# Feed forward 0 of a two-layer trunk: squares of half 2 first, table constants later, each piece's phases behind its C table, and three smaller edits

## The chip, the cores and the metric

The kernel runs on one core of a Trainium2 chip. TensorE multiplies matrices, VectorE, ScalarE and GpSimd work element by element, SyncE issues most DMAs. The profile calls them PE (PEld for its weight loads), DVE, ACT, POOL and SP. The metric is the device time of one execution in microseconds (us), the median of several runs; lower is better.

## The reference

A causal decoder trunk of two layers on x of 1024 tokens by 1024 channels, all in float32. What matters here is the feed forward and the S5 mixer:

```python
for i in range(DEPTH):
    h = h + mix_fns[i % 2](rms_norm(h, norm_mix[i]), *mix_params[i])
    h = h + sqrelu_mlp(rms_norm(h, norm_ffn[i]), *ffn[i])     # square(relu(hn @ up)) @ down, 4096 wide
    gate = jax.nn.sigmoid(rms_norm(h, norm_ple[i]) @ ple[i][0])
    h = h + (p[i] @ ple[i][1]) * gate
return rms_norm(h, norm_final)
```

Mixer 0 is RWKV-7 beside a short convolution. Mixer 1 is S5: 64 groups of 16 channels with 64 complex states each, a diagonal recurrence over time, then a GLU.

## The kernel before, in words

The residual h lies in SBUF as 8 x 2 tiles `h[j][hf]` of 128 channels by 512 tokens; hf 0 ("half 1" of the tokens, named `ha` in the profile) and hf 1 ("half 2", named `h`). Every matrix product is made of three matmuls of float32r parts: high by high, high by low, low by high (`mm3`, L161). The high part is a cast on ACT, the low part a subtraction on DVE or POOL.

The stages run one after the other: mixer 0, feed forward 0, layer 0's gate product (`ple`), S5 with its GLU, feed forward 1, `ple` of layer 1 with the final norm (`finish`).

**Feed forward** (`ffn`, L253) is a list of units k = -6, -5, ... Each unit has 8 slots. In a unit the up product of weight block k+5 takes 24 matmuls, and from k = 0 the down product of block k takes another 21, in a Strassen-like form with sums of the weight's quarters. Work on the other engines is queued with `at(k, slot, f)`: for a down block the four sums `draw` on POOL (L296 to L299), the cast `whi` on ACT (L303), the subtraction `wlo` on DVE (L306), and the load of the next block, one unit ahead of its use. The first units, k = -5 and -4, use channels j 0 to 3 of both halves, units -3 and -2 channels 4 to 7. For the order of instructions: PE's is the order in which the code is written; on the other engines a scheduler of the framework, with its own model of time, orders what is ready, so that work that waits for nothing on PE can float forward.

**Its inputs.** The norm's factor of half 1 is known (r0). Half 1's inputs are scaled before they are split (`scaled`, L192: `xs` on DVE, `prh` on ACT, `prl` on DVE). Half 2's first units run unscaled and its sum of squares is taken meanwhile (`sumsq`, L206: square on ACT, `acc` L215 on POOL); `ps_ms` (L232) adds over the channels on PE, `ps_rs` (L242) spreads the result, and `again` then scales half 2's inputs anew, in place.

**S5's tables** are made beside feed forward 0 and `ple`. `tables()` gives constants (small DVE instructions, L921 to L1089), one step per slot from slot S5_START on. Then 32 pieces of two groups follow, piece n from slot S5_AT + S5_EACH * n, 24 of them in feed forward 0, the rest in `ple`. `s5_piece` makes the C table `CL` (L1145, L1146, L1152), `BL`, and the kernel `kt`; `s5_powers` (L1203 to L1206) makes powers for 16 pieces; `s5_phases` (L1218 to L1222) makes a piece's `phase` table on POOL with a scratch tile `pt`, and a DMA on SP stores it (L1224). SP's queue also carries the weight loads.

**S5's scan** (`s5`, L1333) works on 16 steps of four groups. Step s in the loop does `s5_y(s-2)`, `s5_x(s)`, `s5_t(s+1)` and, every second step, an output or an input transposition. `s5_x` multiplies on PE (`ps_x`, L1280), rotates on DVE (L1286 to L1289), scans on DVE (L1290), and rotates back on POOL with four instructions (L1294 to L1297) into `s5h`. `s5_y` multiplies `s5h` with the C table on PE (L1313).

**finish** (L1385) writes each 128 tokens in two DMAs on SP (L1411, L1412). The second one's tile `ot1` has three buffers.

Of the kernel before, what the change touches and what calls it, by code (L numbers as in the profile page):

```python
# [21 lines left out]
S5_START, S5_PREP, S5_AT, S5_EACH, S5_FFN = -24, 1, 88, 16, 24  # L22
# [3 lines left out]
S5_PH = (1, 2, 4)  # L26
# [36 lines left out]
class Trunk:  # L63
# [189 lines left out]
    def ffn(self, l, xn, rstd, done, hook):  # L253
# [187 lines left out]
    def ple(self, l, xn, rstd, pt, done, side):  # L441
        nc = self.nc
        gate, proj = self.i[f"l{l}_ple_gate"], self.i[f"l{l}_ple_proj"]
        wp = None
        per = -(-len(side) // 13)
        for j0 in range(0, ND, 2):
# [3 lines left out]
            wg = [self.wload(gate[:, j * P:(j + 1) * P].rearrange("(k p) c -> p k c", p=P), 8, P) for j in js]  # L450
# [758 lines left out]
    def s5_phases(self, pc, pool):  # L1209

        nc = self.nc
        G = nc.gpsimd
        E1, E2 = (e[:, pc % 8] for e in self.pw)
        E = pool.tile([P, 2, 16, 8], F32, tag="s5p", name="phase", bufs=1)
        t = pool.tile([P, 2, 16, 8], F32, tag="pt", name="pt", bufs=1)
        hi = E2.rearrange("p n (a o) -> p n a o", o=1).broadcast_to([P, 2, 16, 8])
# [1 line left out]
        G.tensor_mul(E, hi, lo(0))  # L1218
        G.tensor_mul(t, hi, lo(1))
# [1 line left out]
        G.tensor_sub(E[:, 0], E[:, 0], t[:, 1])
        G.tensor_add(E[:, 1], E[:, 1], t[:, 0])  # L1222
# [46 lines left out]
    def s5_x(self, i, q, pool):  # L1269
# [24 lines left out]
        G.tensor_mul(v(t)[:, :, :, f], v(a)[:, :, :, f], cs[:, :, :, f])  # L1294
        G.tensor_mul(v(u)[:, :, :, f], v(a)[:, :, :, f], sn[:, :, :, f])  # L1295
        G.tensor_sub(h[:, 0, :, 1:P], v(t)[:, 0, :, f], v(u)[:, 1, :, f])
        G.tensor_add(h[:, 1, :, 1:P], v(t)[:, 1, :, f], v(u)[:, 0, :, f])  # L1297

    def s5_y(self, i, cj, q):
# [9 lines left out]
        for n in range(2):  # L1309
            for r in range(2):  # L1310
                for g in range(NG):
                    rows = slice(64 * g, 64 * g + 64)
                    nc.tensor.matmul(py[g][:, n * P:(n + 1) * P], h[rows, r, n], w[rows, n, (NG + r) * P:(NG + r + 1) * P],  # L1313
                                     start=False, stop=r == 1, skip_group_check=True)
# [59 lines left out]
    def turn(self, hf, jj, t, scale):  # L1374
# [5 lines left out]
        o = self.xp.tile([P, H], F32, tag="ot%d" % jj, name="ot", bufs=(8, 3)[jj])  # L1380
# [3 lines left out]
    def finish(self):  # L1384
# [7 lines left out]
        def done(j, hf):  # L1392
# [14 lines left out]
            for t in range(4):  # L1407
# [4 lines left out]
                nc.sync.dma_start(rows[:, H:D], self.turn(hf, 1, t, rs[:, t:t + 1]))  # L1412
# [192 lines left out]
    def build(self, layers=(0, 1), stop=None):  # L1605
        tc, nc = self.tc, self.nc
        from contextlib import ExitStack
        with ExitStack() as st:
# [28 lines left out]
            for l in range(2):  # L1637
# [79 lines left out]
                with tc.tile_pool(name=f"pp{l}", bufs=2, reuse_waits="tile") as self.pp, tc.tile_pool(name=f"ep2{l}", bufs=3, reuse_waits="tile") as self.ep:  # L1717
# [5 lines left out]
                    with ExitStack() as s2:  # L1723
# [63 lines left out]
```

## Time and profile before

| | |
|---|---|
| median of 3 runs | 2714.06 us (2712.27 to 2714.18) |
| the profiled execution's own time | 2712.81 us |
| its span, first to last instruction | 2711.0 us |
| PE busy | 2579.0 us (95%) |
| DVE, ACT, POOL busy | 1822.1, 1022.0, 1175.4 us |
| mean granted clock of TensorE | 0.979 |

A row of the timeline has: start, duration, engine, line, operation, output<-inputs, count, and in brackets how long the engine sat idle before and who ended that. A row of grouped instructions has: line, engine, operation, output<-inputs, shapes, count | busy us, mean ns | idle before. A row of windows has: the stretch, its length, the busy us of PE, PEld, DVE, ACT and POOL (with the number of instructions), the granted clock (1.00 is full), the DMA share and GB/s. A row of waits has: who waited, for whom, us in total, times, longest. The times of the profile are counted from the span's start. Matmuls are pipelined, so their durations overlap. A plain float32 matmul stands in the trace as two instructions.

### The profile page before, as it was taken

To read this page: it belongs to the slowest core of one execution; us is meant where nothing else is said; L and a number is where in the kernel's file an instruction comes from. 1 tells how busy PE (TensorE), PEld (TensorE's weight loads), DVE (VectorE), ACT (ScalarE), POOL (GpSimd) and SP (SyncE) were. 2 spreads that over 40 slices of the span, in tenths; PEclk is the share of its full clock that TensorE was granted. 3 is DMA by queue.
4 is the path that set the end of the run, shared out by engine and by line. 5 is a ranking of instruction groups with operands and counts; after the bars stand their busy time and mean duration, and the time that the engine had idled before them with its cause. 6 is when DMAs were issued, how large, how long until landed. Compare 5 with 4: busy or idle time off the path is not lost.

```text
span 2711.0 us, 46747 instructions
## 1 busy us (share of the span) xinstructions
PE 2579.0 (95%) x18781; PEld 2069.7 (76%) x18781; DVE 1822.1 (67%) x2646; ACT 1022.0 (38%) x1705; POOL 1175.4 (43%) x1517
## 2 busy tenths in 40 slices
PE   8998999999779899999999988999999999999998
PEld 5776777777567778888887776788788888888787
DVE  6664665663787677777777659423577787777854
ACT  4334444343333333434344436323333233233432
POOL 5444343443439875545556617211434344343410
PEclk9998999999899999999999989999999999999999
DMA  4223211321212232232222335211111111111121
GB/s 113 60 59 103 80 56 49 111 69 58 78 40 60 74 89 72 72 82 75 73 76 74 107 96 168 67 47 40 49 49 54 48 53 49 55 47 55 44 77 63
DMA packets 273430, 189.04 MB, mean 70 GB/s; under 512 B 33039, under 2 KB 256509, under 8 KB 273213
## 3 DMA queue, kind: packets, MB, share of 16 engines
q1 hardware_dynamic: 264336, 174.50, 22.0%
q10 hardware_dynamic: 7516, 7.10, 0.9%
q0 software_dynamic: 1360, 4.46, 0.5%
q8 instruction: 147, 2.41, 0.4%
q14 instruction: 71, 0.57, 0.1%
HBM read 156.92 MB, written 29.10 MB: 69 GB/s over the span
## 4 chain that ended last, share of the span: by engine, by line
PE 57%; POOL 7%; DVE 4%; issue 2%; DMA 2%; ACT 1%; POOLq 0%; ACTq 0%; SPq 0%; DVEq 0%
PE ps_dnx L380 11%; PE ps_up L164 7%; PE ps_up L166 7%; PE ps_up L165 7%; PE ps_dny L380 5%; PE ps_dnz L380 3%; PE ps_gl L164 2%; PE ps_gl L166 2%; PE ps_gl L165 2%; PE ps_g L164 2%; PE ps_g L165 2%; PE ps_g L166 2%; DMA draw<-in_l_ffn_down_dram 1%; DVE prl L184 1%; POOL zs L1295 1%
## 5 line engine op out<-in xcount | busy, mean ns | idle before, releaser
L165 PE MATMUL ps_up<-prl,uwh 128*128 128x512 f32 x1024 | 405.2, 396 | 2.8 <-DVE prl L184 2.8
L164 PE MATMUL ps_up<-prh,uwh 128*128 128x512 f32 x1024 | 406.5, 397 | 1.4 <-ACT prh L183 1.4
L166 PE MATMUL ps_up<-prh,uwl 128*128 128x512 f32 x1024 | 406.1, 397 | 0.0
L296 POOL TENSOR_TENSOR draw<-draw 128x128 f32<-128x128 f32 x120 | 70.2, 585 | 465.5 <-DMA draw<-in_l_ffn_down_dram 375.9
L283 POOL TENSOR_TENSOR uwl<-uraw,uwh 128x512 fp32r<-128x512 f32 x136 | 183.8, 1352 | 168.8 <-ACT uwh L280 162.3
L165 PEld LDWEIGHTS ps_up<-prl,uwh 128*128 128x128 f32 x1024 | 194.0, 189 | 48.7 <-DVE prl L184 3.5
L164 PEld LDWEIGHTS ps_up<-prh,uwh 128*128 128x128 f32 x1024 | 194.3, 190 | 47.1 <-ACT prh L183 1.8
L166 PEld LDWEIGHTS ps_up<-prh,uwl 128*128 128x128 f32 x1024 | 194.2, 190 | 45.2
L383 DVE TENSOR_TENSOR h<-h,ps_dnx 128x512 f32<-128x512 f32 x240 | 164.6, 686 | 85.0 <-PE ps_dnx L380 84.3
L280 ACT CAST uwh<-uraw 128x512 fp32r<-128x512 f32 x136 | 84.4, 620 | 360.7 <-PE ps_up L165 339.3
L380 PE MATMUL ps_dnx<-hidh,whi 128*128 128x512 f32 x480 | 193.0, 402 | 23.8 <-DVE ha L383 20.7
L153 POOL TENSOR_TENSOR wlo<-wraw,whi 128x1024 fp32r<-128x1024 f32 x66 | 158.4, 2400 | 124.3 <-ACT whi L152 120.6
L215 POOL TENSOR_TENSOR acc<-acc,sq 128x512 f32<-128x512 f32 x70 | 103.7, 1489 | 228.5 <-ACT sq L214 225.5
L380 PE MATMUL ps_dnx<-hidl,whi 128*128 128x512 f32 x480 | 189.2, 394 | 5.9 <-DVE hidl L345 5.9
L380 PE MATMUL ps_dnx<-hidh,wlo 128*128 128x512 f32 x480 | 188.8, 393 | 0.0
L164 PE MATMUL ps_z<-prh,whi 128*128 128x512 f32 x416 | 179.2, 431 | 7.5 <-ACT whi L152 6.7
L383 DVE TENSOR_TENSOR ha<-ha,ps_dnx 128x512 f32<-128x512 f32 x240 | 163.7, 682 | 15.3 <-PE ps_dnx L380 15.3
L166 PE MATMUL ps_z<-prh,wlo 128*128 128x512 f32 x416 | 166.8, 401 | 6.6 <-POOL wlo L153 6.6
L152 ACT CAST whi<-wraw 128x1024 fp32r<-128x1024 f32 x104 | 108.8, 1047 | 165.7 <-PE ps_z L165 59.5
L165 PE MATMUL ps_z<-prl,whi 128*128 128x512 f32 x416 | 165.7, 398 | 0.8 <-DVE prl L506 0.8
L345 DVE TENSOR_TENSOR hidl<-r_up,hidh 128x512 fp32r<-128x512 f32 x188 | 151.9, 820 | 8.1 <-ACT hidh L353 2.8
L383 DVE TENSOR_TENSOR ha<-ha,ps_dny 128x512 f32<-128x512 f32 x120 | 82.5, 687 | 108.8 <-PE ps_dny L380 108.7
(447 smaller groups left out, 6318.3 us busy)
## 6 DMA issues: line engine op xcount, KB each, us to landing
uraw<-in_l_ffn_up_dram SPq DMA_DIRECT2D x128, 256.0 KB
draw<-in_l_ffn_down_dram SPq DMA_DIRECT2D x120, 256.0 KB
wraw<-in_l_w_in_dram SPq DMA_DIRECT2D x52, 512.0 KB
s5w<-s5w SPq DMA_DIRECT2D x32, 384.0 KB
wraw<-in_l_w_out_dram SPq DMA_DIRECT2D x16, 512.0 KB
wraw<-in_l_ple_gate_dram SPq DMA_DIRECT2D x16, 512.0 KB
wraw<-in_l_glu_w_dram SPq DMA_DIRECT2D x16, 512.0 KB
toep<-kt SPq DMA_DIRECT2D x32, 240.0 KB
```

What stands on the lines that cost most here:

```text
L152: nc.scalar.copy(hi[:, :n], raw[:, :n])
L153: self.lo_engine().tensor_sub(lo[:, :n], raw[:, :n], hi[:, :n].bitcast(F32))
L164: nc.tensor.matmul(ps, wh, xh, start=start, stop=False)
L165: nc.tensor.matmul(ps, wh, xl, start=False, stop=False)
L166: nc.tensor.matmul(ps, wl, xh, start=False, stop=stop)
L215: (eng or nc.vector).tensor_add(acc, acc, sq)
L280: A.copy(uw[m][0], raws["u"])
L283: nc.gpsimd.tensor_sub(uw[m][1], raws["u"], uw[m][0].bitcast(F32))
L296: G.tensor_add(raw[:, 4], raw[:, 0], raw[:, 2])
L345: return lambda: eng.tensor_sub(st[nm][1], t, st[nm][0].bitcast(F32))
L380: nc.tensor.matmul(ps, w[:, a], v, start=id(ps) not in begun, stop=n == 2, skip_group_check=True)
L383: V.tensor_add(hv, hv, ps)
```

## The change

- `done` takes parts: "x" makes the split inputs, "s" the square and its sum. In feed forward 0, half 2 comes first with both for channels 0 to 3, then its squares for 4 to 7, then half 1's inputs 0 to 3, then the inputs 4 to 7 of half 2 and of half 1.
- Where `eng` is POOL, the last two of the eight sums go to DVE. This holds for both feed forwards and both `ple`.
- `ps_ms` and `ps_rs` come a unit later, and the new scaling with them.
- The table constants start 16 slots later, the pieces 16 slots later and with a step of 15 instead of 16. A piece's phases come at its slots 3, 4 and 6 instead of 1, 2 and 4.
- The phases' scratch tile shares the one buffer of the C table's scratch tile (`tmp`), so that it is free only when the C table of the piece in progress has been added up.
- `ffn` calls `after` in its last two full units, which loads and splits the first two gate blocks for `ple`.
- S5's rotation back: POOL makes `t` whole and half of `u`, DVE the other half of `u` with its sign, straight into the operands of PE, and PE adds what POOL added before: 16 matmuls with the C table per step instead of 8.
- `finish`: a fourth buffer for `ot1`, and the second DMA of each 128 tokens goes to POOL's queue.

```diff
-S5_START, S5_PREP, S5_AT, S5_EACH, S5_FFN = -24, 1, 88, 16, 24
+S5_START, S5_PREP, S5_AT, S5_EACH, S5_FFN = -8, 1, 104, 15, 24
-S5_PH = (1, 2, 4)
+S5_PH = (3, 4, 6)
...
-            st["acc"][hf] = self.sumsq(s, st["acc"][hf], eng=eng)
+            st["acc"][hf] = self.sumsq(s, st["acc"][hf], eng=eng if st["n"][hf] < ND - 2 else None)
...
+        for k in range(2):
+            at(ND_ + k, 7, after)
...
-        t = pool.tile([P, 2, 16, 8], F32, tag="pt", name="pt", bufs=1)
+        t = pool.tile([P, 2, 16, 8], F32, tag="tmp", name="pt", bufs=1)
...
-        G.tensor_mul(v(t)[:, :, :, f], v(a)[:, :, :, f], cs[:, :, :, f])
-        G.tensor_mul(v(u)[:, :, :, f], v(a)[:, :, :, f], sn[:, :, :, f])
-        G.tensor_sub(h[:, 0, :, 1:P], v(t)[:, 0, :, f], v(u)[:, 1, :, f])
-        G.tensor_add(h[:, 1, :, 1:P], v(t)[:, 1, :, f], v(u)[:, 0, :, f])
+        t, u = q["h"] = self.s5h[i % 2]
+        f = slice(0, P - 1)
+        G.tensor_mul(t[:, :, :, 1:P], v(a)[:, :, :, f], cs[:, :, :, f])
+        G.tensor_mul(u[:, 0, :, 1:P], v(a)[:, 0, :, f], sn[:, 0, :, f])
+        V.scalar_tensor_tensor(u[:, 1, :, 1:P], v(a)[:, 1, :, f], -1.0, sn[:, 1, :, f], ALU.mult, ALU.mult)
...
-        for n in range(2):
-            for r in range(2):
-                for g in range(NG):
-                    rows = slice(64 * g, 64 * g + 64)
-                    nc.tensor.matmul(py[g][:, n * P:(n + 1) * P], h[rows, r, n], w[rows, n, (NG + r) * P:(NG + r + 1) * P],
-                                     start=False, stop=r == 1, skip_group_check=True)
+        for m in range(2):
+            for n in range(2):
+                for r in range(2):
+                    for g in range(NG):
+                        rows = slice(64 * g, 64 * g + 64)
+                        nc.tensor.matmul(py[g][:, n * P:(n + 1) * P], h[m][rows, r ^ m, n], w[rows, n, (NG + r) * P:(NG + r + 1) * P],
+                                         start=False, stop=m == r == 1, skip_group_check=True)
...
-        o = self.xp.tile([P, H], F32, tag="ot%d" % jj, name="ot", bufs=(8, 3)[jj])
+        o = self.xp.tile([P, H], F32, tag="ot%d" % jj, name="ot", bufs=(8, 4)[jj])
...
-                nc.sync.dma_start(rows[:, H:D], self.turn(hf, 1, t, rs[:, t:t + 1]))
+                nc.gpsimd.dma_start(rows[:, H:D], self.turn(hf, 1, t, rs[:, t:t + 1]))
...
-                            for js in range(0, 4), range(4, 8):
-                                for hf in (1, 0):
-                                    for j in js:
-                                        ffn_done(j, hf)
+                            for js, hf, parts in ((range(0, 4), 1, "xs"), (range(4, 8), 1, "s"), (range(0, 4), 0, "x"),
+                                                  (range(4, 8), 1, "x"), (range(4, 8), 0, "x")):
+                                for j in js:
+                                    ffn_done(j, hf, parts)
...
-                            at(-5, 6, lambda: next(ffn_in["r"]))
-                            at(-4, 4, lambda: scale1(ffn_in))
+                            at(-4, 6, lambda: next(ffn_in["r"]))
+                            at(-3, 2, lambda: scale1(ffn_in))
                             for j in range(ND):
-                                at(-3, 2 * j + j // 4 * 5, lambda j=j: again(ffn_in, j))
+                                at(-3, 4 + 2 * j + j // 4, lambda j=j: again(ffn_in, j))
```

Where the instructions stand now, first on POOL in feed forward 0. Before, where one block's weights are summed (`draw`, at 899 us of the profile), `uwl` is the low part of an up block, and `phase` and `pt` belong to pieces whose C tables come later:

```order
L296 TENSOR_TENSOR draw<-draw 128x128
L297 TENSOR_TENSOR draw<-draw 128x128
L1219 TENSOR_TENSOR pt<-E_11982,E_11981 128x256
L298 TENSOR_TENSOR draw<-draw 128x128
L1218 TENSOR_TENSOR phase<-E_11982,E_11981 128x256
L299 TENSOR_TENSOR draw<-draw 128x128
L1221 TENSOR_TENSOR phase<-phase,pt 128x128
L1222 TENSOR_TENSOR phase<-phase,pt 128x128
L1219 TENSOR_TENSOR pt<-E_11982,E_11981 128x256
L283 TENSOR_TENSOR uwl<-uraw,uwh 128x512
```

A whole phase table and the start of the next stand beside the four sums of one block there. In the changed kernel a piece on POOL reads so (its lines are numbered 4 to 12 higher):

```order
L1156 TENSOR_TENSOR CL<-LR,cx 128x288
L1190 TENSOR_TENSOR kt<-kt,sk 128x2x16
L1163 TENSOR_TENSOR CL<-CL,tmp 128x288
L1188 TENSOR_TENSOR sk<-dT,eye_9240 128x32
L1231 TENSOR_TENSOR pt<-E_10470,E_10469 128x256
L1233 TENSOR_TENSOR phase<-phase,pt 128x128
L1234 TENSOR_TENSOR phase<-phase,pt 128x128
L1157 TENSOR_TENSOR tmp<-LI,cx 128x288
L300 TENSOR_TENSOR draw<-draw 128x128
```

One phase table now follows each C table, and the next comes a piece later. The second place is PE in S5's scan, two steps, each with its product with `toep`, its product with `s5h`, and the next `ps_x`. Before:

```order
L1307 MATMUL ps_y<-toep,U 128x128 x4
L1313 MATMUL ps_y<-s5w,s5h_16893 128x128 x8
L1280 MATMUL ps_x<-U,s5w 64x128 x8
L1260 MATMUL ps_u_17132<-ident,Z 128x128 x4
L1328 MATMUL ps_y_17143<-ident,Y 128x128 x4
L1328 MATMUL ps_y_17149<-ident,Y 128x128 x4
```

And in the changed kernel:

```order
L1318 MATMUL ps_y<-toep,U 128x128 x4
L1325 MATMUL ps_y<-s5w,s5h_16894 128x128 x8
L1325 MATMUL ps_y<-s5w,s5k_16895 128x128 x8
L1292 MATMUL ps_x<-U,s5w 64x128 x8
L1272 MATMUL ps_u_17140<-ident,Z 128x128 x4
L1340 MATMUL ps_y_17151<-ident,Y 128x128 x4
```

A second group of eight matmuls, with `s5k` (the `u` of the code), has come ahead of `ps_x`. On DVE the new half product follows the scan directly:

```order
L1300 TENSOR_TENSOR xa<-xa,xc 128x256
L1301 TENSOR_TENSOR xa<-xa,xc 128x256
L1302 SCALAR_TENSOR_TENSOR xa<-rc,xa 128x512
L1308 SCALAR_TENSOR_TENSOR s5k_16895<-xa,s5w 128x2x127
L859 TENSOR_TENSOR prl<-y,prh 128x512 x2
```

It stands ahead of the two `prl` and of the next step's `xa`, which take up DVE's queue behind it.

More of the change, by code (lines that the diff above doesn't have):

```diff
@@ L174, in prep, with done @@
         st = {"xn": [{}, {}], "n": [0, 0], "acc": [None, None], "rstd": [known.get(0), known.get(1)]}
-        def done(j, hf):
+        def done(j, hf, parts="xs"):
             nc = self.nc
             s = self.hv(j, hf)
-            if split and hf in known:
+            if "x" not in parts or not split:
+                pass
+            elif hf in known:
                 st["xn"][hf][j] = self.scaled(s, gain, j, known[hf])
-            elif split:
+            else:
                 xn = self.pair(self.prp, [P, H], "pr")
@@ L185, in done @@
                 st["xn"][hf][j] = xn
-            if hf in known:
+            if hf in known or "s" not in parts:
                 return
-            st["acc"][hf] = self.sumsq(s, st["acc"][hf], eng=eng)
+            st["acc"][hf] = self.sumsq(s, st["acc"][hf], eng=eng if st["n"][hf] < ND - 2 else None)
             st["n"][hf] += 1
@@ L246, in rstd_steps, with ffn @@
         yield out
-    def ffn(self, l, xn, rstd, done, hook):
+    def ffn(self, l, xn, rstd, done, hook, after):
         nc = self.nc
@@ L439, in load_p, with gate, ple @@
         return pt
-    def ple(self, l, xn, rstd, pt, done, side):
+    def gate(self, l, j):
+        gate = self.i[f"l{l}_ple_gate"]
+        return self.wload(gate[:, j * P:(j + 1) * P].rearrange("(k p) c -> p k c", p=P), 8, P)
+    def ple(self, l, xn, rstd, pt, done, side, first):
         nc = self.nc
-        gate, proj = self.i[f"l{l}_ple_gate"], self.i[f"l{l}_ple_proj"]
+        proj = self.i[f"l{l}_ple_proj"]
         wp = None
@@ L449, in ple @@
                 wp = self.wload(proj[:, j0 * P:j0 * P + 512].rearrange("(k p) c -> p k c", p=P), 2, 512, self.pp)
-            wg = [self.wload(gate[:, j * P:(j + 1) * P].rearrange("(k p) c -> p k c", p=P), 8, P) for j in js]
+            wg = [self.gate(l, j) for j in js] if j0 else first
             ps = {}
@@ L1339, in s5 @@
             nc.gpsimd.memset(self.later[:, 0:1], 0.0)
-            self.s5h = [pool.tile([P, 2, 2, P], F32, name=f"s5h{n}") for n in range(2)]
-            for t in self.s5h:
+            view = lambda t: t.rearrange("p (r n c) -> p r n c", r=2, n=2)
+            self.s5h = [(pool.tile([P, 2, 2, P], F32, name=f"s5h{n}"),
+                         view(self.np_.tile([P, H], F32, tag="sq", name=f"s5k{n}", bufs=4))) for n in range(2)]
+            for t in self.s5h[0] + self.s5h[1]:
                 nc.gpsimd.memset(t[:, :, :, 0:1], 0.0)
@@ L1649, in build @@
                     self.up = s2.enter_context(tc.tile_pool(name=f"up{l}", bufs=2, reuse_waits="tile"))
-                    hook = None
+                    hook, first = None, []
                     if l == 0:
@@ L1708, in build @@
                     with tc.manual_schedule(engines={mybir.EngineType.PE}):
-                        self.ffn(l, st["xn"], st["rstd"], done2, hook)
+                        self.ffn(l, st["xn"], st["rstd"], done2, hook, lambda: first.append(self.gate(l, len(first))))
                 if l == 0:
@@ L1728, in build @@
                             side = [g for _, g in sorted(side, key=lambda q: q[0])]
-                        self.ple(l, st2["xn"], rstd, pt, done1, side)
+                        self.ple(l, st2["xn"], rstd, pt, done1, side, first)
                 s1.close()
```

2 lines of the change are left out of this document (removed).

## The prediction

> **What bounds the kernel now.** I read the page first: PE is busy for 2579.0 of 2711.0 us, so little is left outside a few stretches. Its timeline of 40 slices shows them by the granted clock and the busy share, and I cut those stretches by the table of windows (columns: length, then busy us and instructions of PE, PEld, DVE, ACT, POOL, granted clock, DMA share, GB/s). The rows are the head of feed forward 0 in two parts, units 4 to 16, the steady rest, and S5's scan:
>
> ```profile
> 721.00:745.00 24.00, 12.89 (x37) 9.58 (x38) 22.01 (x25) 12.52 (x22) 11.14 (x8) 0.71 0.11 33
> 745.00:819.00 74.00, 60.17 (x244) 46.31 (x243) 65.05 (x177) 27.97 (x45) 26.06 (x42) 0.91 0.14 39
> 819.00:966.00 147.00, 132.25 (x553) 104.46 (x553) 101.45 (x139) 47.50 (x77) 132.25 (x246) 0.97 0.24 70
> 966.00:1450.00 484.00, 481.59 (x2157) 392.32 (x2156) 369.24 (x553) 191.97 (x329) 249.63 (x360) 1.00 0.27 75
> 1614.00:1712.00 98.00, 78.57 (x769) 66.23 (x770) 87.60 (x99) 56.97 (x112) 69.20 (x60) 0.93 0.48 143
> ```
>
> The fourth row is feed forward at its best: 2157 matmuls in 484 us, 4.46 a us. At that rate the 37, 244 and 553 matmuls of the rows above would take 8.3, 54.8 and 124 us. So the first 24 us lose 15.7, the next 74 lose 19.2, and units 4 to 16 lose 23. That is 58 us in all, the most that the change's first two parts can win.
>
> In the third row POOL is busy 132.25 of 147 us, the steady rest half its time. The waits of that stretch (who waits, for whom, us, times, longest) and POOL's groups in it say with what:
>
> ```profile
> ACT whi L303 <- POOL draw L299: 25.2, 9, 4.9
> DVE wlo L306 <- ACT whi L303: 15.4, 7, 4.2
> PE ps_dnx L380 <- DVE ha L383: 12.9, 8, 3.8
> ```
>
> ```profile
> L1218 POOL TENSOR_TENSOR phase<-E,E 128x256 f32<-128x256 f32 x20 | 15.3, 764 | 5.1 <-DMA s5w<-phase 4.9
> L1219 POOL TENSOR_TENSOR pt<-E,E 128x256 f32<-128x256 f32 x21 | 14.3, 682 | 0.8
> L1221 POOL TENSOR_TENSOR phase<-phase,pt 128x128 f32<-128x128 f32 x20 | 11.6, 582 | 0.7
> L1222 POOL TENSOR_TENSOR phase<-phase,pt 128x128 f32<-128x128 f32 x20 | 10.1, 507 | 0.0
> ```
>
> Twenty pieces' phases, 51.3 us in all and 2.56 us a piece, sit among the weights' sums. The cast waits for the sums, the subtraction for the cast, and PE behind them for the adds on DVE. The pitch of a unit can be read from what comes once in each: `wlo` at both ends of twelve units here (timeline), and six matmuls in a row, two units apart, in the steady rest (the chain of waits that ended last: start, duration, what):
>
> ```profile
> 819.16 1.53 DVE L306 TENSOR_TENSOR wlo<-draw,whi 128x896 fp32r<-128x896 f32 x1
> 966.76 1.08 DVE L306 TENSOR_TENSOR wlo<-draw,whi 128x896 fp32r<-128x896 f32 x1
> ...
> 1097.22 1.38 PE ps_dnx L380 x6
> 1118.70 1.38 PE ps_dnx L380 x6
> ```
>
> That is 147.6 / 12 = 12.3 us a unit against 21.48 / 2 = 10.74.
>
> **The change, part by part**, against the profiled span of 2711.0.
>
> *A, the head.* DVE is busy 22.01 of 24 us, then 65.05 of 74. The timeline shows where PE and DVE stood for half 2's sum of squares, and what one add costs on DVE (a final-norm add) and when the last table constant was done:
>
> ```profile
> 741.06 1.87 PE L232 MATMUL ps_ms<-meanw,acc 128*128 128x1 f32 x8 [8.33 <-POOL acc L215]
> 752.47 0.82 DVE L199 SCALAR_TENSOR_TENSOR xs<-h,cv,rstd 128x512 f32<-128x512 f32 x1 [8.18 <-ACT rstd L244]
> 813.67 0.96 DVE L1089 COPY wk<-lv 64x448 f32<-64x448 f32 x2
> 2676.04 0.69 DVE L215 TENSOR_TENSOR acc<-acc,sq 128x512 f32<-128x512 f32 x1 [0.76 <-ACT sq L214]
> ```
>
> PE stood 8.33 us in front of `ps_ms` with a matmul queue behind it. Now all squares of half 2 come before half 1's inputs and `ps_ms` stands a unit later, so PE's wait should go. What comes late next is DVE: the splits take it nearly whole. Its idle 8.18 I take to shrink to 3 (−5); two adds move onto it (+1.4); the constants start two units later but in the order end behind the fifth `wlo` instead of the fourth, one unit, where DVE has 101.45 busy of 147, worth some −3 of the 19.2. Sum −7. Ends: −2, if DVE's idle time is only passed on; −11, if DVE's 8.2 and the 3 go whole and the adds are hidden.
>
> *B, units 4 to 16.* At one piece in 15 slots, twelve units (96 slots) hold 6.4 pieces instead of 20: 13.6 × 2.56 = 35 us leave POOL, 132 to 97. Twelve units of the steady pitch are 129 us, so POOL is no longer the bound, and the pitch can fall to 10.74: 12 × 1.56 = 18.7. I take −16, since constants now fall into the first of these units. Ends: −23, the whole loss; −4, if the 12.9 that PE waits for DVE's adds and the constants keep most of it.
>
> *C, the steady rest* takes these phases, 51.3 us onto 249.63 of 484. The place where one could hurt is the weight's chain:
>
> ```profile
> 1105.08 0.79 POOL L299 TENSOR_TENSOR draw<-draw 128x128 f32<-128x128 f32 x1
> 1108.17 0.94 ACT L303 CAST whi<-draw 128x896 fp32r<-128x896 f32 x1 [0.81 <-PE ps_dnx L380]
> 1109.15 1.09 DVE L306 TENSOR_TENSOR wlo<-draw,whi 128x896 fp32r<-128x896 f32 x1
> ```
>
> The sums end at 1105.87, 2.3 us before ACT may start (it waits for PE to free the buffer), and `wlo` is ready at 1110.24 for the unit that starts near 1118.8: another 8 us. A phase table of 2.56 us in front of the sums costs 0.26 of those 8. I take +1; ends 0 and +5 (20 × 0.26, all shown).
>
> *D, the two starts of `ple`* and their norms:
>
> ```profile
> 1472.15 0.50 PE L166 MATMUL ps_g<-prh,wlo 128*128 128x512 f32 x1 [1.62 <-DVE wlo L153]
> 1483.41 1.05 PE L232 MATMUL ps_ms<-meanw,acc 128*128 128x1 f32 x8 [2.27 <-POOL acc L215]
> ...
> 2574.06 0.50 PE L166 MATMUL ps_g<-prh,wlo 128*128 128x512 f32 x1 [0.89 <-DVE wlo L153]
> 2582.51 1.05 PE L232 MATMUL ps_ms<-meanw,acc 128*128 128x1 f32 x8 [0.85 <-POOL acc L215]
> ...
> L215 POOL TENSOR_TENSOR acc<-acc,sq 128x512 f32<-128x512 f32 x70 | 103.7, 1489 | 228.5 <-ACT sq L214 225.5
> ```
>
> Blocks split two units earlier remove 1.62 and 0.89. The loads, casts and subtractions go into units where POOL is half idle, so they cost nothing; uncovered, they would cost what they save. The last two adds take 0.69 on DVE instead of 1.49 on POOL, 1.6 less of 2.27, and all 0.85. Sum −5; ends 0 and −6.
>
> *E, S5's scan.* Two steps take 12.90 us. The window of two steps, PE's product with `s5h` and what follows it, one of POOL's groups, and one shape on DVE beside POOL:
>
> ```profile
> 1658.10:1671.00 12.90, 9.87 (x106) 8.28 (x104) 12.43 (x15) 8.17 (x16) 10.02 (x8) 1.00 0.57 164
> 1669.87 1.20 PE L1313 MATMUL ps_y<-s5w,s5h 64*128 64x128 f32 x16
> 1671.00 1.09 PE L1280 MATMUL ps_x<-U,s5w 128*64 128x128 f32 x16
> ...
> L1294 POOL TENSOR_TENSOR zc<-xa,s5w 128x508 f32<-128x508 f32 x15 | 21.5, 1432 | 66.7 <-DVE xa L1290 62.2 <-PE ps_x L1280 2.8 <-issue 1.7
> ...
> 1661.04 0.43 DVE L1288 TENSOR_TENSOR xa<-xa,xc 128x256 f32<-128x256 f32 x1
> 1661.14 1.46 POOL L1295 TENSOR_TENSOR zs<-xa,s5w 128x508 f32<-128x508 f32 x1
> 1661.39 1.49 DVE L1289 TENSOR_TENSOR xa<-xa,xc 128x256 f32<-128x256 f32 x1
> ...
> 1669.42 0.94 DVE L1289 TENSOR_TENSOR xa<-xa,xc 128x256 f32<-128x256 f32 x1
> ```
>
> DVE is full, 12.43 of 12.90, partly because it stands: the same shape took 0.43 us, and 1.49 while `zs` ran on POOL until 1662.60, and 0.94 a step later: 1.57 too much in the pair. After the change POOL has 1.43 and about half of 1.46 a step instead of 10.02 / 2 = 5.01, so these delays can go; DVE gets a product of 254 elements, between 0.43 (the free 256) and 1.49. With free ones DVE needs 12.43 − 1.57 + 0.86 = 11.7. PE gets 16 more matmul rows a step at 1.13 (1671.00 − 1669.87): 9.87 + 2.26 = 12.1 of 12.9. So PE sets the pair at 12.1 to 12.3: −0.6 in 7.5 pairs, −4. Ends: −9 (DVE's 11.7 sets it, the products overlapping on PE) and +10 (the first rival).
>
> *F, the end.*
>
> ```profile
> out_dram<-ot SPq DMA_DIRECT2D x16, 256.0 KB
> ...
> GB/s 0 0 9 0 0 0 0 0 0 0 0 0 0 0 0 0 0 0 0 0 61 391 379 379 375 386 389 375 382 382 384 372 396 145 0 0 9 0 0 0
> ...
> 2704.33 0.75 DVE L1381 SCALAR_TENSOR_TENSOR ot<-ps_ft,frs,gbc 128x512 f32<-128x512 f32 x1 [0.63 <-DMA out_dram<-ot]
> ...
> rscr<-rstd POOLq DMA_DIRECT2D x1, 256.0 KB, 2.3
> ```
>
> The second row is the DMA rate from 2680 to 2715 in 40 slices: 4.2 MB go out at about 380 GB/s, 11 us without a gap. A fourth buffer lets DVE run ahead of a transfer that sets the end all the same. I take 0; ends −2.3 (three to four waits like the one shown) and +2.3 (a transfer of POOL's queue lands later by the whole of the one that the trace has).
>
> Sum: −7 − 16 + 1 − 5 − 4 + 0 = −31. The span becomes 2680. The profiled execution's own time lies 1.8 above its span (2712.81), the median of the runs 1.25 above that (2714.06). So 2680 + 1.8 + 1.25 = **2683 us**.
>
> **The rivals.**
>
> *R1, DVE behind POOL in the scan.* The new product reads two SBUF operands (`xa`, `s5w`) right after the scan, when POOL's whole product of the same scan starts. If POOL comes first every time, DVE stands 1.43 in each step. DVE's pair of steps is then 12.43 − 1.57 + 2 × 1.43 = 13.7; with today's 0.47 between busy and period it is 14.2, +1.3 in 7.5 pairs: the stage is 10 longer instead of 4 shorter, 2697. For it: the 1.49. Against: POOL also waits for the scan, and DVE, which has just ended it, is first in its own queue. It decides when the product's mean passes 0.79 (12.43 − 1.57 + 2 × 0.79 + 0.47 = 12.9).
> The Trainium skill (SBUF — State Buffer, "Who interferes with whom") says that a DVE instruction with two SBUF inputs and a GpSimd instruction that reads SBUF share one pair of ports, that whichever starts first holds it for the whole instruction, and that the other blocks fully. By that rule, the trace agrees (0.43 against 1.49, with `L1289` ending after `zs`), and this edit moves work to exactly that pair; the sum by the rule at its worst would be R1's.
>
> *R2, DVE instead of POOL in units 4 to 16.* The constants, two units later, and the adds hold PE, and B brings −4: 2695. For it: the wait of 12.9 on DVE's adds. Against: DVE is busy 69% there, and its own waits (15.4) come from POOL.
>
> *R1 and R2 together*: 2683 + 14 + 12 = 2709, just inside no change as it is bounded below.
>
> *R3, slower: SP's queue.* Each piece's phase table is stored by SP, and the loads of up and down blocks are queued behind. Before, the tables were done long ahead; now each store waits for POOL, which waits for the C table of its piece. From a delay of about 10 us a piece (2.3 + 8, C above) it reaches PE. At 12 us it costs 24 × 2 = 48 instead of winning: 2683 + 48 = 2731. For it: the store now stands behind DVE's and POOL's chain in every piece. Against: the three slots 3, 4, 6 leave the phases time to be done before SP comes to the store, and POOL has half of its time free.
>
> *The phases float forward anyway*: excluded by the order, in which each waits for the shared scratch tile.
>
> **How the numbers follow.** 0.2%, 5.4 us, is about what a measurement of this kernel can tell from no change. Forecast 0.65, R1 alone 0.11, R2 alone 0.11, both 0.04, R3 0.04, and 0.05 for more gain than the ends allow. So faster 0.65 + 0.11 + 0.11 + 0.05 = 0.92, same 0.04, slower 0.04. Low end: A, B, C, D and F at their ends, 2683 − 4 − 7 − 1 − 1 − 2.3, some 2667. High end: R1 with C at its end, 2697 + 4 = 2701; R2 lies inside. The two together and R3 are left out.
>
> **What would show it.** In the changed profile POOL's share between units 4 and 16 is near 75% with some 6 phase tables, and twelve `wlo` take about 131 us (−16); `ps_ms` waits under 1 us; the steady rest keeps 4.46 matmuls a us; two steps of the scan take 12.1 to 12.3 with the new product at 0.4 to 0.8 us. I am wrong on the main term if the pitch stays above 12 with POOL under 80% (R2), on the scan if it takes more than 12.9 (R1), and wrong altogether if waits for `draw` or `uraw` loads show on PE after 966 us (R3).

## The result, and the profile after

| | before | changed |
|---|---|---|
| median of 4 runs | 2713.16 us (2712.2 to 2714.18) | 2692.17 us (2690.77 to 2694.0) |
| ratio, 95% interval | | 0.9924, 0.9912 to 0.9936 |
| profiled execution, its span | 2711.0 us | 2692.2 us |
| PE, DVE, ACT, POOL busy | 2579.0, 1822.1, 1022.0, 1175.4 us | 2586.8, 1829.3, 1021.3, 1136.5 us |

The changed kernel is 21.0 us (0.8%) faster. The forecast was 2683, a gain of 30; the result lies inside the range and 9 us above that forecast. The windows of the changed kernel, cut as before:

```profile
721.00:745.00 24.00, 18.75 (x64) 12.76 (x64) 20.59 (x27) 11.52 (x21) 13.64 (x6) 0.79 0.12 33
745.00:819.00 74.00, 60.44 (x245) 46.12 (x244) 70.98 (x185) 29.79 (x48) 27.31 (x33) 0.93 0.16 45
819.00:966.00 147.00, 145.88 (x635) 117.34 (x634) 111.49 (x159) 54.84 (x87) 83.30 (x135) 1.00 0.23 62
966.00:1450.00 484.00, 472.87 (x2099) 381.26 (x2098) 374.93 (x538) 189.38 (x327) 312.99 (x484) 1.00 0.28 78
1614.00:1712.00 98.00, 94.40 (x1018) 82.37 (x1017) 73.22 (x104) 60.16 (x112) 31.55 (x28) 0.99 0.46 138
```

Read the counts of PE. The first stretch now holds 64 matmuls instead of 37, the third 635 instead of 553, with POOL at 83 us instead of 132. But the fourth, the long steady rest, holds 2099 instead of 2157: time won early is given back there. The same with a marker that comes once per unit, the `wlo` of a block (timelines, first of before and then of the changed kernel: the 4th, the 19th and the 60th and last of feed forward 0):

```profile
809.82 1.08 DVE L306 TENSOR_TENSOR wlo<-draw,whi 128x896 fp32r<-128x896 f32 x1
992.93 1.40 DVE L306 TENSOR_TENSOR wlo<-draw,whi 128x896 fp32r<-128x896 f32 x1 [0.73 <-ACT whi L303]
1431.71 1.09 DVE L306 TENSOR_TENSOR wlo<-draw,whi 128x896 fp32r<-128x896 f32 x1
```

```profile
801.79 1.09 DVE L310 TENSOR_TENSOR wlo<-draw,whi 128x896 fp32r<-128x896 f32 x1
963.45 1.08 DVE L310 TENSOR_TENSOR wlo<-draw,whi 128x896 fp32r<-128x896 f32 x1
1421.26 1.08 DVE L310 TENSOR_TENSOR wlo<-draw,whi 128x896 fp32r<-128x896 f32 x1
```

The changed kernel leads by 8.0 us at the 4th, by 29.5 at the 19th, and by only 10.5 at the 60th. Between the last two, 457.8 us instead of 438.8, it loses 19.0. All experiments below are read by these markers, and by the first and last scan of S5. The columns of this table are the time up to the 4th `wlo`, from there to the 19th, from there to the 60th ("the rest"), to the first scan (the first `ple` and what lies around it), and from the first to the last scan; all of the profiled execution, in us. Each ratio is to runs of the kernel before on the same chip. The column "to 4th" holds mixer 0 as well, which no edit here touches and which alone differs by up to 5 us between the profiles (feed forward 0 begins between 717.8 and 723.2 us), so small differences in it say nothing:

| kernel | median | ratio to before, 95% | to 4th | to 19th | rest | to scan | scan |
|---|---|---|---|---|---|---|---|
| before | 2713.16 | | 809.8 | 183.1 | 438.8 | 186.8 | 94.9 |
| changed | 2692.17 | 0.9924 (0.9912 to 0.9936) | 801.8 | 161.7 | 457.8 | 179.9 | 88.4 |
| e1 step 16 | 2692.13 | 0.9927 (0.9912 to 0.9942) | 803.1 | 160.9 | 453.5 | 181.6 | 86.8 |
| e2 phases float | 2714.45 | 1.0009 (0.9999 to 1.0018) | 802.4 | 182.4 | 451.9 | 188.4 | 87.9 |
| e3 T3 on DVE | 2683.47 | 0.9900 (0.9883 to 0.9916) | 799.3 | 162.2 | 452.6 | 178.8 | 88.4 |
| e4 fewer powers | 2689.00 | 0.9916 (0.9901 to 0.9930) | 805.1 | 161.4 | 454.4 | 178.7 | 86.8 |
| e5 step 16, float | 2703.89 | 0.9961 (0.9946 to 0.9976) | 801.6 | 180.4 | 439.1 | 189.6 | 87.2 |
| e6 step 16, T3 on DVE | 2684.47 | 0.9889 (0.9869 to 0.9909) | 798.5 | 162.2 | 449.7 | 181.2 | 86.8 |
| e7 T3 on DVE, output on SP | 2682.98 | 0.9885 (0.9870 to 0.9900) | 803.0 | 162.8 | 452.2 | 178.9 | 88.3 |
| e8 before, shared scratch | 2710.05 | 0.9988 (0.9978 to 0.9997) | 812.0 | 163.3 | 454.6 | 184.1 | 94.9 |
| e9 as e6, fewer powers | 2674.84 | 0.9861 (0.9846 to 0.9876) | 801.6 | 162.4 | 439.0 | 181.8 | 88.4 |
| e10 before, new rotation | 2708.62 | 0.9985 (0.9976 to 0.9995) | 807.7 | 181.7 | 439.6 | 186.7 | 86.8 |
| e11 before, new head | 2707.95 | 0.9987 (0.9976 to 0.9998) | 806.9 | 179.3 | 439.6 | 189.5 | 93.3 |
| e12 as e6, powers spread | 2680.06 | 0.9883 (0.9861 to 0.9905) | 797.9 | 162.9 | 446.4 | 181.2 | 86.8 |

Where did the 19 us go? The waits of the changed kernel between its 19th and 60th `wlo` have PE wait for nobody but DVE's adds, 11 waits and 11 us in all; the kernel before has none there. The longest of these waits, 2.69 us, can be followed back in the timeline (start, duration, engine; the bracket is the idle time ahead and who ended it):

```profile
1072.78 1.74 POOL L287 TENSOR_TENSOR uwl<-uraw,uwh 128x512 fp32r<-128x512 f32 x1
1074.48 0.67 POOL L1216 TENSOR_TENSOR E<-E,pq 128x16 f32<-128x16 f32 x1
...
1076.44 0.25 POOL L1217 TENSOR_TENSOR E<-E,pq 128x32 f32<-128x32 f32 x1
1076.65 1.29 POOL L355 TENSOR_TENSOR r_up<-r_up 128x512 f32<-128x512 f32 x1
...
1077.97 0.62 ACT L357 CAST hidh<-r_up 128x512 fp32r<-128x512 f32 x1 [4.55 <-POOL r_up L355]
...
1079.51 1.66 DVE L349 TENSOR_TENSOR hidl<-r_up,hidh 128x512 fp32r<-128x512 f32 x2 [2.91 <-ACT hidh L357]
...
1081.10 0.84 DVE L1165 TENSOR_TENSOR BL<-BL,tmp 128x256 f32<-128x256 f32 x1
...
1081.86 0.68 DVE L387 TENSOR_TENSOR h<-h,ps_dnx 128x512 f32<-128x512 f32 x1
...
1082.59 0.79 PE L384 MATMUL ps_dnx<-hidh,whi 128*128 128x512 f32 x1 [2.69 <-DVE h L387]
```

Read it upwards. PE waits for the add `h`, which stands in DVE's queue behind a sum for `BL` and `hidl`; `hidl` waits for `hidh`; and ACT stands 4.55 us for one subtraction, `r_up`, that POOL makes once in four units (the sum T3 of the Strassen-like form). POOL makes it late because the powers of the second set of eight pieces (`E`, `pq`, 28 instructions, 9.4 us of work between 1063 and 1080) stand in front of it, and with them the feed forward's own `uwl`, 1.74 us. (One set of powers serves eight pieces, not 16 as the description of the kernel says.) In the kernel before the second set was done by 885 us, and with no phases or powers left in the rest:

```profile
884.64 0.32 POOL L1206 TENSOR_TENSOR E<-E,pq 128x64 f32<-128x64 f32 x1
```

### The profile page after: what moved, and what is told of

It is laid out like the page before. It is cut to its first block, busy times and chain, and to the rows that moved or that the text cites. A ratio compares the mean times of both kernels' runs of the same rounds, so it can differ in the third digit from the quotient of the medians.

```text
span 2692.2 us, 47213 instructions
## 1 busy us (share of the span) xinstructions
PE 2586.8 (96%) x19037; PEld 2077.8 (77%) x19037; DVE 1829.3 (68%) x2676; ACT 1021.3 (38%) x1705; POOL 1136.5 (42%) x1481
## 4 chain that ended last, share of the span: by engine, by line
PE 75%; DVE 12%; issue 4%; POOL 4%; ACT 3%; DMA 1%; SPq 0%; POOLq 0%; ACTq 0%; DVEq 0%
PE ps_dnx L384 11%; PE ps_up L166 7%; PE ps_up L164 7%; PE ps_up L165 7%; PE ps_dny L384 5%; PE ps_z L164 3%; PE ps_z L166 3%; PE ps_z L165 3%; PE ps_dnz L384 3%; PE ps_gl L164 2%; PE ps_gl L165 2%; PE ps_gl L166 2%; PE ps_g L164 2%; PE ps_g L165 2%; PE ps_g L166 2%
## 5 line engine op out<-in xcount | busy, mean ns | idle before, releaser
L287 POOL TENSOR_TENSOR uwl<-uraw,uwh 128x512 fp32r<-128x512 f32 x136 | 188.4, 1385 | 223.5 <-ACT uwh L284 223.3
L219 POOL TENSOR_TENSOR acc<-acc,sq 128x512 f32<-128x512 f32 x56 | 82.9, 1483 | 193.5 <-ACT sq L218 190.2
```

Of the source, the lines that this page charges most:

```text
L219: (eng or nc.vector).tensor_add(acc, acc, sq)
L287: nc.gpsimd.tensor_sub(uw[m][1], raws["u"], uw[m][0].bitcast(F32))
```

## The experiments

Three theories began. **T1**: the step of 15 slots walks the pieces through the units of 8 slots, and some places don't fit. **T2**: POOL's queue; its subtraction for T3 comes late behind phases and powers, whatever the step. After the first four runs came **T3**: both costs are there, and each alone is enough for most of the loss; with **T4** as its rival, something else in the change. (T1 to T4 in bold are theories. "T3's subtraction" is named after a sum T3 in the code and is another thing.)

**e1**, the step back to 16:

```diff
-S5_START, S5_PREP, S5_AT, S5_EACH, S5_FFN = -8, 1, 104, 15, 24
+S5_START, S5_PREP, S5_AT, S5_EACH, S5_FFN = -8, 1, 104, 16, 24
```

> The changed kernel with one number back: a piece every 16 slots instead of 15 (first piece still at slot 104). The changed kernel gives back 19 us between units 18 and 59 of feed forward 0. Theory T1 (the step of 15 walks the pieces through the units, and some places don't fit): at least two thirds of the 19 us go, the time is 2676 to 2680. Theory T2 (POOL's queue: once in four units its subtraction r_up, on which ACT, DVE and PE wait, stands behind phases or powers, whatever the step): within 4 us of the changed kernel, 2688 to 2696.

The median is the same, and the rest still loses 453.5 − 438.8 = 14.7 us. T1 alone falls.

**e2**, the scratch tile back in its own buffer:

```diff
-        t = pool.tile([P, 2, 16, 8], F32, tag="tmp", name="pt", bufs=1)
+        t = pool.tile([P, 2, 16, 8], F32, tag="pt", name="pt", bufs=1)
```

> The changed kernel with the phases' scratch tile in a buffer of its own again, so that phases can float ahead; step, start and slots stay as changed. T2: the steady rest wins back some 12 of its 19 us, since POOL is free of phases there, and units 4 to 16 lose 12 to 16: 2688 to 2697. T1: the rest keeps its loss (15 or more of the 19) and units 4 to 16 lose 12 to 16 on top: 2701 to 2710.

2714.45, outside both expectations. Units 4 to 18 take 182.4 us again: what was won there hangs on this one line. The rest still loses 13.1 with POOL free of phases and powers, so T2 alone falls too; and the first `ple` loses 8.5 against the changed kernel, which neither theory had.

**e3**, T3's subtraction on DVE:

```diff
-                diff(G, 1, 3, 1, "T3")
+                diff(V, 1, 3, 1, "T3")
```

> The changed kernel with the one subtraction of feed forward that POOL makes once in four units (r_up for T3, both layers) on DVE instead; the sum is the same. T2: the wait of ACT for POOL's r_up is gone; 11 us of PE's waits shrink to 3, 2682 to 2687. T1: the tables' own work on DVE still collides, and DVE has 0.7 us more every four units: 2690 to 2698.

The median is 9 us lower, as T2 said, though the two intervals of the ratios touch. In the profiles 5.2 us are won in the rest (452.6) and 3.5 between the last scan and the last `ps_g`, where feed forward 1 has the same subtraction; of the 2.5 ahead of the 4th `wlo` 1.8 lie in mixer 0. What remains in the rest, 13.8, is not this subtraction.

**e4**, the powers of the second and third set left out:

```diff
+        if n in (1, 2):
+            for k in range(7):
+                yield
+            return
```

> The changed kernel without the powers for the second and third set of eight pieces (the 56 POOL instructions near 1060 to 1080 and 1220 to 1260 us); later phases are made from the first set's powers, so that work is left out. T2: the two longest stalls (PE's 2.69 and 1.87 us and the slow matmuls behind each) go, 4 to 8 us less: 2684 to 2688. T1: 0 to 2 us less, 2690 to 2692.

2689.0, 3 us less: between the two, and its interval overlaps that of the changed kernel. In the rest 3.4 us of the 19 go.

**e5**, both e1's and e2's edits:

> The changed kernel with both numbers of the last two experiments back: a piece every 16 slots, and the phases' scratch tile in a buffer of its own. With each alone the rest of feed forward 0 still lost 13 to 15 us of the 19. Theory T3 (two costs, each alone enough: the step of 15 for pieces whose phases are ahead, phases and powers in the rest for any step): with both back the rest loses 0 to 4 us, units 4 to 16 gain nothing, 2698 to 2703. Rival T4 (something else of the change, the start at slot 104, the slots 3, 4, 6 or the head, costs some 13 us in the rest): the rest still loses 10 or more, 2708 to 2715.

The rest takes 439.1 us, the loss is 0.3: T3 holds and T4 falls, though the median lies 0.9 above T3's range. These two windows of equal length, first the changed kernel, then e5, show it in one row each:

```profile
965.00:1425.00 460.00, 448.87 (x1994) 361.48 (x1993) 355.01 (x513) 174.42 (x302) 304.20 (x477) 1.00 0.29 80
```

```profile
965.00:1425.00 460.00, 458.19 (x2056) 373.38 (x2055) 355.59 (x529) 180.94 (x311) 238.34 (x349) 1.00 0.28 76
```

2056 matmuls against 1994, and 128 POOL instructions fewer. But units 4 to 18 lose their 19 us, and the total is 12 us slower than the changed kernel.

The trace of e2 shows in part how the step of 15 costs without phases and powers. In its rest PE waits ten times, 7.8 us in all, each time for an add on DVE; e5 has one such wait, 0.2 us. The longest:

```profile
1367.21 1.39 DVE L1165 TENSOR_TENSOR BL<-BL,tmp 128x256 f32<-128x256 f32 x1
...
1370.54 1.54 DVE L310 TENSOR_TENSOR wlo<-draw,whi 128x896 fp32r<-128x896 f32 x1
1372.01 0.67 DVE L387 TENSOR_TENSOR ha<-ha,ps_dnx 128x512 f32<-128x512 f32 x1
...
1372.83 0.48 PE L384 MATMUL ps_dnx<-hidh,whi 128*128 128x512 f32 x1 [1.68 <-DVE ha L387]
```

DVE has no idle time ahead of that add: a piece's `BL` and the block's `wlo` stand there, and both take long (the same `BL` line took 0.42 us at 1142, and `wlo` takes 1.08 elsewhere).

**e6**, the step 16 and T3's subtraction on DVE:

> The changed kernel with a piece every 16 slots and T3's subtraction on DVE. T3: the POOL part of the cost at step 16 goes with it, the rest loses 4 to 9 instead of 14.7: 2682 to 2687. T4: nothing in it has to do with POOL's subtraction: 2689 to 2694.

The median agrees with T3, the size in the rest does not: it loses 10.9, more than the 4 to 9 expected. That loss is not spread. The kernel's lead over the kernel before falls from 31.5 to 26.5 us between the 28th and the 32nd `wlo`, from 26.7 to 21.7 between the 45th and the 48th, and is flat elsewhere. The first place, in its timeline:

```profile
1074.69 0.74 POOL L1217 TENSOR_TENSOR E<-E,pq 128x16 f32<-128x16 f32 x1
1075.39 0.91 POOL L300 TENSOR_TENSOR draw<-draw 128x128 f32<-128x128 f32 x1
...
1077.39 0.29 POOL L1215 TENSOR_TENSOR pq<-E,wk 128x64 f32<-128x64 f32 x1
...
1078.48 0.46 POOL L303 TENSOR_TENSOR draw<-draw 128x128 f32<-128x128 f32 x1
```

```profile
1078.97 0.94 ACT L307 CAST whi<-draw 128x896 fp32r<-128x896 f32 x1 [2.76 <-POOL draw L303]
...
1079.95 1.09 DVE L310 TENSOR_TENSOR wlo<-draw,whi 128x896 fp32r<-128x896 f32 x1 [1.90 <-ACT whi L307]
1080.95 0.68 DVE L387 TENSOR_TENSOR ha<-ha,ps_dnx 128x512 f32<-128x512 f32 x1
...
1081.78 0.47 PE L384 MATMUL ps_dnx<-hidh,whi 128*128 128x512 f32 x1 [1.63 <-DVE ha L387]
```

This is the chain of the prediction's part C, sums, cast, subtraction. Powers from 1066 us on stand in front of and among the sums; the cast waits 2.76 for them, `wlo` 1.90 for the cast; and the add that PE waits for stands behind `wlo` in DVE's queue. The prediction had `wlo`'s slack right (PE waits for no `wlo` in this rest) and missed what is queued behind it.

This first stall is less than half of the place. Two units later PE stands again, 2.18 us (2.28 at the second place), and there the same chain begins with a load:

```profile
1101.23 0.46 POOL L300 TENSOR_TENSOR draw<-draw 128x128 f32<-128x128 f32 x1 [3.12 <-DMA draw<-in_l_ffn_down_dram]
...
1103.10 0.94 ACT L307 CAST whi<-draw 128x896 fp32r<-128x896 f32 x1 [1.99 <-POOL draw L303]
1104.07 1.18 DVE L310 TENSOR_TENSOR wlo<-draw,whi 128x896 fp32r<-128x896 f32 x1 [2.64 <-ACT whi L307]
...
1105.90 0.51 PE L384 MATMUL ps_dnx<-hidh,whi 128*128 128x512 f32 x1 [2.18 <-DVE ha L387]
```

SP issued that load late, at 1098.04. Before 1083 its queue had stood 11.7 us for POOL's `uwl`, which came behind the powers. In e9 below, level with e6 to under 1 us at this point, SP stands 5.8 us at most in this stretch, the load goes out at 1094.88, and PE does not wait. That SP's long wait is what made the load late is inferred from this comparison.

**e9**, e6 without the powers of sets two and three, with e4's edit:

> The changed kernel with a piece every 16 slots, T3's subtraction on DVE, and without the powers of the second and third set of eight pieces (that work is left out). With step 16 and the subtraction on DVE the rest of feed forward 0 still lost 11 us, nearly all in two places of 5 us, where these powers stand. If the powers' bursts on POOL are that cost: the rest loses 0 to 3 us, 2673 to 2677. If the phases among the weights' sums are: the rest keeps 7 or more, 2680 to 2685.

The rest takes 439.0: nothing is lost, and PE has no idle time in the window of e9:

```profile
965.00:1425.00 460.00, 460.00 (x2066) 375.77 (x2065) 369.49 (x551) 184.91 (x316) 257.79 (x396) 1.00 0.29 81
```

So at step 16 the loss of 14.7 is T3's subtraction (3.8, e1 to e6) and the two sets of powers with what they hold up (10.7, e6 to e9). The phases themselves, still in the rest here, cost nothing once those two are gone. e9 leaves the powers' work out as well as their burst; only e12 bears on which of the two it is.

**e12**, e6 with all work kept and the powers spread (`E2` is taken when its first step comes, `self.pw` set at the last step):

```diff
-S5_POW = (-8, -7, -5, -4, -2, -1, 0)
+S5_POW = (-24, -20, -16, -9, -6, -3, 0)
...
-        E1 = pool.tile([P, 8, 2, 8], F32, tag="E1", name="E1", bufs=1)
+        E1 = pool.tile([P, 8, 2, 8], F32, tag="E1", name="E1", bufs=2)
```

> Step 16 and T3's subtraction on DVE, all work kept, the powers spread: the small ones (E1, now with two buffers) from 24 slots ahead of their set, the large ones over the last 9 slots and not in one unit. If the bursts are the cost, part of the 10 us goes: 2677 to 2682. If the amount of work is, or the scheduler packs them again: 2683 to 2687.

2680.06, and 3.3 of the 10.9 us in the rest come back. The lead still drops by 5 at the second set's place and now by 2.3 at the third's: in the order 17 and 16 instructions of the powers still follow each other at the two places with no weight's sum between them. Of the kernels that keep all the work it has the lowest median, but its interval overlaps with those of e3, e6 and e7.

**e7**, e3 with the output's second DMA back on SP:

```diff
-                nc.gpsimd.dma_start(rows[:, H:D], self.turn(hf, 1, t, rs[:, t:t + 1]))
+                nc.sync.dma_start(rows[:, H:D], self.turn(hf, 1, t, rs[:, t:t + 1]))
```

> The changed kernel with T3's subtraction on DVE and the second DMA of each 128 tokens of the output back on SP's queue (the fourth buffer stays). The end of the changed kernel came 2.4 us later against its last ps_g matmuls than before. If that is POOL's queue: 2 to 3 us under the run with the subtraction alone, 2680 to 2682. If it is noise of the one profile: 2683 to 2684.

The medians differ by 0.5, less than the spread of the runs. The profiles settle it: from the last `ps_g` matmul to the end, the nine kernels with the second DMA on POOL's queue take 19.4 to 19.6 us (19.5 in the changed kernel), the five with it on SP's take 18.1 to 18.2, this one among them, with its fourth buffer. The queue costs some 1.3 us. (The 2.4 of the expectation holds from the last `ot` on, 6.9 against 4.5 us; with the fourth buffer and SP's queue it is 6.0.)

**e8**, the kernel before with the shared scratch tile alone (e2's line, the other way):

> The kernel before with one line of the change: the phases' scratch tile shares the C table's buffer. Units 4 to 16 should win 16 to 21 us (the step of the prediction), as the run with the line undone lost them. T3: the rest pays 10 to 15 of it back, since phases and powers come into it at step 16 too: 2703 to 2710. T1 (the step is what costs): the rest pays 0 to 4: 2692 to 2700.

Units 4 to 18 win 19.8 us and the rest gives 15.8 back, a little over the 10 to 15 expected, at the old step of 16. This one line is most of the change's gain and most of its loss.

**e10**, the kernel before with the new rotation alone (the scan's part of the change's diff):

> The kernel before with one part of the change: S5's rotation back, half of a product on DVE, 16 matmuls instead of 8. The forecast said -4. From the changed trace: the scan 6 to 8 us shorter, of which the start of the GLU may give back some: 2705 to 2709. The rival on record (DVE standing behind POOL): 2713 or more.

The scan is 8.1 us shorter, and 3.8 of that are lost between the last scan and the last `ps_g`, all of it before the first `wlo` of feed forward 1. The net is about −4 (interval 0.9976 to 0.9995).

**e11**, the kernel before with the new head alone (parts of `done`, the order of the inputs, `ps_ms` and `again` later, two adds on DVE):

> The kernel before with one part of the change: half 2's squares first, ps_ms and the new scaling a unit later, the last two sums on DVE; the tables stay early. Forecast for the head: -7 of which -3 from the later tables. If the order of the squares carries it: 2703 to 2707. If the later tables do: 2709 to 2713.

2707.95 lies between the two. Up to the 4th `wlo` it wins 2.9, where the changed kernel wins 8.0. But mixer 0 is in these numbers. From the first `ps_up` matmul of feed forward 0 to the 4th `wlo` it takes 84.9 us, before 88.9 and the changed kernel 81.2: 4.0 won of 7.7.

## Why the forecast had the sign right and the gain too large

By the forecast's own parts, in the two profiles (span −18.8, forecast −31; the profiled run of the changed kernel, 2694.0, is the slowest of its four):

- **A, the head, −7 forecast: −8.0.** Of this, 0.3 lies in mixer 0. The size is right, and so is the split: counted from the first `ps_up`, the new order gives 4.0 (e11; −5 + 1.4 forecast) and the tables that come later the other 3.7, by difference (3 forecast). `ps_ms` no longer has any wait, and DVE's idle time ahead of `xs` is 3.22, forecast 3:

```profile
742.44 0.95 PE L236 MATMUL ps_ms<-meanw,acc 128*128 128x1 f32 x8
...
747.12 1.42 DVE L203 SCALAR_TENSOR_TENSOR xs<-h,cv,rstd 128x512 f32<-128x512 f32 x2 [3.22 <-ACT rstd L248]
```

- **B, units 4 to 16, −16 forecast: −20.8** over the same twelve units (147.6 to 126.8 us), −21.4 over units 4 to 18, near the ceiling of 23. POOL went from 132 to 83 us of 147, further than the 97 forecast: three whole phase tables and the start of a fourth are left there, not six, and the powers of two later sets went with them. e2 and e8 show that the shared tile does it, alone. R2 (DVE keeps the pitch) is refuted.
- **C, the steady rest, +1 forecast with ends 0 and +5: +19.0.** This is the step that failed. It costed what moved as "these phases, 51.3 us", 2.56 at a time, against one chain with 2.3 and 8 us of slack. e9 shows that at step 16 the phases do cost nothing there. What was left out: the powers must move with the phases, since their two tiles are held until the eight pieces' phases are made, and they come as 28 instructions, 9.4 us of work within 16; once in four units POOL also makes a subtraction of the feed forward itself, with little slack; and DVE, in order, stands at `wlo` with PE's adds behind it, as SP, in order, stands with the loads. At step 16 powers and subtraction are the whole loss. The step of 15, which the sum for C gave no cost, is a further one: with phases and powers ahead (e2) the rest loses 13.1 at step 15 and 0.3 at step 16 (e5). Its waits are for adds that stand behind table work in DVE's queue; why that work falls worse at step 15 was not taken apart, and the 19.0 of the changed kernel are not a plain sum of these costs.
- **D, the starts of `ple`, −5 forecast: −6.9 up to the first scan,** only in part by what I named. PE's waits for `wlo` in front of `ps_g` (1.62 and 0.89) are gone in the changed kernel, e2 and e5, which have the early gate blocks, and stand unchanged in e8 and e11, which have not. The waits in front of `ps_ms` went from 2.27 to 1.60 and from 0.85 to 0.18. But e2 and e5 have 188.4 and 189.6 us there, more than before (186.8), and so has e11 (189.5): in these three PE stands 4.5, 4.9 and 5.7 us in front of a piece's product until ACT's `rstd` is done, where before has 0.6 and the kernels with the shared tile have no such wait. The tile alone gives 2.7 (e8). The early blocks alone were not run, and the size of each part stays open.
- **E, the scan, −4 forecast: −6.5,** and a loss of 3.7 between its end and the last `ps_g`, 2.5 of it before the first `wlo` of feed forward 1; alone, in e10, −8.1 and +3.8. What the scan's end passes on there was not followed. The new product takes 0.46 us and POOL's half product 0.90 in the mean:

```profile
L1308 DVE SCALAR_TENSOR_TENSOR s5k<-xa,s5w 128x254 f32<-128x254 f32 x15 | 6.9, 458 | 0.5
```

```profile
L1306 POOL TENSOR_TENSOR s5h<-xa,s5w 128x508 f32<-128x508 f32 x16 | 22.4, 1403 | 84.1 <-DVE xa L1302 33.2 <-PE ps_y L1325 33.0 <-PE ps_y L1318 14.7
L1307 POOL TENSOR_TENSOR s5k<-xa,s5w 128x254 f32<-128x254 f32 x15 | 13.5, 903 | 0.0
```

  R1 (DVE standing behind POOL) needed a mean over 0.79 and is refuted. Two steps take 11.8 us in the mean (10.7 to 12.3 but for one pair of 14.2), under my 12.1 to 12.3; in this pair PE is busy 11.29 of 11.94 and DVE 11.26, so PE does not bound it alone, as I had it:

```profile
1639.26:1651.20 11.94, 11.29 (x142) 9.96 (x140) 11.26 (x18) 8.11 (x16) 4.55 (x4) 1.00 0.58 177
```

- **F, the end, 0 forecast: +1.4,** inside its ends, and by the cause named for the worse end, POOL's queue (e7).
- **R3** (loads late on SP's queue) did not come as it was priced: PE itself waits for no load in the rest of the changed kernel. A small form of it is real, though: about half of PE's idle time in e6 (4.46 of 8.05 us) reaches it through loads that SP issued late, which had stood chiefly for `uwl` (11.7 us at a time) and less for the store of a phase (1.5).

The sum: −8.0 − 21.4 + 19.0 − 6.9 − 6.5 + 3.7 + 1.4 = −18.7. C was 18 us too good; B, D, E and A gave 11 back, and the loss after the scan and F took 5. That the result lay in the range is in part luck, by errors of opposite sign.

## What to carry to other kernels

When a shared buffer holds work back, list everything that is chained to that work by its own buffers (here the powers behind the phases) and price the longest run of instructions that will now arrive at once, not the mean. A slack must be read for each kind of work on the engine, the rare ones too (once in four units), and for what is queued behind the waiting instruction, on DVE and on the queue of the loads, not only for the value that it makes. An early gain and a late loss can come from one line: markers that come once in each unit show both, where the total shows only the difference.

## What the runs showed of the hardware

After the idle time of 2.69 us above, PE ran slowly (windows of the changed kernel, granted clock in the third column from the end):

```profile
1079.50:1083.00 3.50, 0.81 (x3) 0.41 (x2) 3.49 (x5) 1.07 (x3) 3.50 (x6) 0.94 0.00 0
1083.00:1086.50 3.50, 3.50 (x10) 2.74 (x10) 2.14 (x4) 0.91 (x1) 3.50 (x7) 0.57 0.01 3
1086.50:1090.00 3.50, 3.50 (x16) 2.83 (x16) 3.35 (x3) 0.03 (x1) 3.42 (x5) 1.00 0.49 117
```

The clock averaged 0.57 over those 3.5 us (0.50 in the stretches of 1 us inside), in which 10 matmuls ran instead of 16, though the row counts PE as fully busy. The Trainium skill (TensorE: Matmul & The Clock Gate, Part 1) has the clock halve after an idle window of about 3.4 us. The drop agrees; here it came after 2.69 us. In e1 it came twice, after 1.87 and 2.19 us, and yet idle times of 1.87 (the changed kernel at 1264.60) and of 2.18 and 2.28 (e6) left it at 1.00: in these runs the length of the gap alone does not decide.

A stall costs more than its idle time even where the clock holds. Of the 19 us lost 11.1 are idle (457.81 − 446.68), and the clock's one drop is worth 1.7. In e6, with five waits and the clock at 1.00 throughout, PE is counted busy for 2.7 us more than before; in e2, with ten, for 5.4. From these two I estimate some 0.5 us a stall, and eleven of them are about the 6 us that are left.

The mean of 0.90 us for POOL's product of 254 elements hides two values, 0.72 and 1.18 us; the 508 elements take 1.37 in the median. In the slow steps DVE's `prl`, with two tiles as inputs (`y`, `prh`), is already running. Where POOL is first, it keeps its 0.72, and DVE's `xa` of 256 elements, which starts beside it, takes 0.68 instead of 0.42:

```profile
1653.97 0.72 POOL L1307 TENSOR_TENSOR s5k<-xa,s5w 128x254 f32<-128x254 f32 x1
1654.29 0.68 DVE L1300 TENSOR_TENSOR xa<-xa,xc 128x256 f32<-128x256 f32 x1
...
1657.43 2.83 DVE L859 TENSOR_TENSOR prl<-y,prh 128x512 fp32r<-128x512 f32 x2
1658.54 1.18 POOL L1307 TENSOR_TENSOR s5k<-xa,s5w 128x254 f32<-128x254 f32 x1
```

The small powers on POOL vary in the same way. `E<-E,pq` of 128x16 took 0.23 us at 1068.05, when DVE stood idle, and 0.67 at 1074.48, while DVE's `r_up` of two tiles ran until 1075.06:

```profile
1068.05 0.23 POOL L1216 TENSOR_TENSOR E<-E,pq 128x16 f32<-128x16 f32 x1
...
1073.88 1.18 DVE L355 TENSOR_TENSOR r_up<-r_up 128x512 f32<-128x512 f32 x1
```
